# The second block's experts in a fixed order on TensorE, four at a time, with one sum for four experts

## The chip, the cores and the metric

The kernel runs on one core of one Trainium2 chip. A core has TensorE (matrix multiplication, PE in the profile; PEld is its weight load), VectorE (DVE), ScalarE (ACT), GpSimd (POOL), and SyncE (SP), which here starts the transfers from the chip's memory. The metric is the device time of one execution in microseconds (us); less is better.

## The reference

Two transformer-like blocks are run one after the other on 256 tokens of width 1024. The change lies in the last stage of the second block, its mixture of experts: each token chooses 2 of 32 experts, and each expert is a gated two-layer network with three float32 weight matrices (`w1`, `w3`: 1024 x 512; `w2`: 512 x 1024).

```python
def expert_block(args):
    xb, e = args
    hid = jax.nn.silu(xb @ w1[e]) * (xb @ w3[e])
    return hid @ w2[e]
...
out = jax.ops.segment_sum(ys * row_gate[:, None], row_tok, num_segments=T)
```

The result is scaled by a gate vector (`g2`), added to the token stream `h`, and a last root-mean-square norm gives the output.

## The kernel before

The token stream `x` lies in the on-chip memory as 8 tiles of 128 channels x 256 tokens. `experts2` goes over the 32 experts in pairs. All experts' weights are read, 6 MB for a pair, in tiles of 1 MB (128 x 2048 float32): four of `w1`, four of `w3`, four of `w2`. `S.load` takes them through a ring of buffers, one transfer on SP's queue for each, in the order of the program; a tile's transfer can start when the matmuls of the tile that held its buffer are done. The ring has 19 buffers in this stage: 4 of the whole program, 7 of the second block, and 8 that `block2` adds at its end with `S.extra_ring(8, S.ring_n)`.

For every four experts ("a group" below):

- `oh` (VectorE) holds one-hot columns that say which token stands in which of an expert's 64 places. `S.gather_parts` multiplies the token rows (kept as a sum of two parts, `u2h` and `u2l`) with `oh`: 32 matmuls `gx`, evacuated from the accumulators (PSUM) by ScalarE and VectorE into `xg`.

For every pair in the group:

- `G` and `U` (64 places x 512 for each of the two experts) take 16 matmuls each. The two experts use the two halves of the array's columns, so their matmuls are 128x64; in the trace each of them has two records.
- `hs` = silu(G) * U (ScalarE, then VectorE); four transposes to `hT` on TensorE, evacuated by VectorE.
- `sg`: the pair's columns of `oh` transposed (evacuated to `sel`), and the gates for its places (`gs`).
- `Yp`: the second layer in two halves `n` of 512 channels, with 8 matmuls (16 records) each; each half is evacuated to a high part `ysh` (ScalarE) and the rest `ysl` (VectorE), both times the gate.
- `add`: for each of the 8 channel tiles, two matmuls `cmb` bring the experts' rows back to their tokens, and VectorE adds the product to `x`.

The accumulators have 8 banks: two for `G`/`U`, two for `Yp`, two (`pt`) for `gx`, `sg` and `hT`, and two (`px`) for `cmb`. No order is written by hand: the framework's scheduler orders each engine's instructions when the program is built, and it may put a pair's `cmb` and the next group's `gx` among the matmuls of `Yp` and of the next pair's `G`. A matmul of 128x128 (`gx`, `cmb`, `sg`, `hT`) uses all columns of the array, one of 128x64 half of them.

In the last pair the squares of the finished tiles of `x` are summed at once (`sums.step`), and `last_norm` writes the output.

Of the kernel before, what the change touches and what calls it, by code (L numbers as in the profile page):

```python
# [173 lines left out]
class K:  # L174
# [123 lines left out]
    def across(self, out, r):  # L298

        for t in range(2):  # L300
            self.nc.tensor.matmul(out[:, 128 * t:128 * t + 128], bc(r[:, t:t + 1], [128, 128]), self.c("ident"), start=True, stop=True)
        return out[:, 0:256]
# [55 lines left out]
                self.split(hi[:, t, a], lo[:, t, a], o, nc.gpsimd)  # L358
        return hi, lo

    def gather_parts(self, pt, xt, oh, n, xg, A, B):

        nc = self.nc
        c = 512 // n
        for k in range(8):
            if k % c == 0:
                p = pt.tile([128, 512], F32, name="gx", tag="tp")
            q = p[:, n * (k % c):n * (k % c) + n]
            for i in range(4):
                nc.tensor.matmul(q, xt[i % 2][:, i // 2, 128 * k:128 * k + 128], oh[:, i // 2], start=(i == 0), stop=(i == 3))  # L370
# [77 lines left out]
def bc(ap, shape):  # L448
    return ap.to_broadcast(shape)
# [912 lines left out]
def block2(S, x):  # L1362

    nc, tc, I = S.nc, S.tc, S.I
    st = ExitStack()
    ring = S.extra_ring(1)
    h1 = S.pool("p2s", st=st, side="right")
# [19 lines left out]
    A = sb.tile([128, 8], F32, name="fgA")  # L1387
# [281 lines left out]
    for i in range(4):  # L1669
# [3 lines left out]
        for fb in range(2):  # L1673
# [43 lines left out]
def experts2(S, x, ring, out):  # L1717

    nc, tc, I = S.nc, S.tc, S.I
    st = ExitStack()  # L1720
    sb = S.pool("m2", st=st, side="right")
    C, V = S.c, S.v
    ident = C("ident")
    M = S.modT2
    CAP = S.cap
    B2 = M[:, 24:32, 0]

    def mm(o, l, r, a=True, b=True):
# [16 lines left out]
    r, ge = S.route  # L1745
# [61 lines left out]
    for e0 in range(0, 32, 2):  # L1807
        if e0 % 4 == 0:

            oh = lb.tile([128, 2, 4, 64], F32R, name="oh", bufs=1)  # L1810
            for t in range(2):
                nc.vector.tensor_tensor(oh[:, t], bc(pos[:, t, e0:e0 + 4, None], [128, 4, 64]), bc(C("iota")[:, None, 0:64], [128, 4, 64]), op=ALU.is_equal)
                if CAP < 64:
                    nc.vector.memset(oh[:, t, :, CAP:].bitcast(F32), 0.0)
            xg = lb.tile([128, 8, 256], F32, name="xg", bufs=1)
            S.gather_parts(pt, ut, oh.rearrange("p t e s -> p t (e s)"), 256, xg, S.A22, B2)
        if e0 == 0:

            nc.vector.tensor_scalar(og, pos, float(CAP), None, op0=ALU.is_gt)
            ov = lb.tile([128, 1], F32, name="ov")  # L1820
            nc.vector.tensor_reduce(ov, og, axis=AX.XY, op=ALU.add)
            nc.vector.tensor_tensor(og, og, gate, op=ALU.mult)
            p = pt.tile([128, 512], F32, name="ov", tag="tp")
            mm(p[:, 0:1], C("ones"), ov)
            nc.vector.tensor_copy(ovi, p[:, 0:1])
        c0 = e0 % 4
        G = pg.tile([128, 512], F32, name="G", tag="G")
        U = pg.tile([128, 512], F32, name="U", tag="G")
        for wn, p in (("w1", G), ("w3", U)):
            for k in range(0, 8, 2):  # L1830
                wt = S.load(I[wn][2 * e0 + k // 2], wn)
                for kk in range(2):
                    for e in range(2):
                        lo = 1024 * kk + 512 * e
                        mm(p[64 * e:64 * e + 64, :], xg[:, k + kk, 64 * (c0 + e):64 * (c0 + e) + 64], wt[:, lo:lo + 512], k + kk == 0, k + kk == 7)

        p = pt.tile([128, 512], F32, name="sg", tag="tp")
        ohp = [oh[:, t, c0:c0 + 2].rearrange("p e s -> p (e s)").bitcast(F32) for t in range(2)]
        for t in range(2):
            nc.tensor.transpose(p[:, 128 * t:128 * t + 128], ohp[t], ident)  # L1840
        for t in range(2):
            mm(p[:, 256:258], ohp[t], gate[:, t, e0:e0 + 2], t == 0, t == 1)
        sel = lb.tile([128, 256], F32R, name="sel", tag="h1", bufs=3)
        nc.scalar.copy(sel, p[:, 0:256])
        gs = lb.tile([128, 1], F32, name="gs", bufs=2)
        for e in range(2):
            nc.vector.tensor_copy(gs[64 * e:64 * e + 64, :], p[64 * e:64 * e + 64, 256 + e:257 + e])
        hs = lb.tile([128, 512], F32, name="hs", tag="h2", bufs=6)
        nc.scalar.activation(hs, G, AF.Silu)
        nc.vector.tensor_tensor(hs, hs, U, op=ALU.mult)  # L1850
        tp = pt.tile([128, 512], F32, name="hT", tag="tp")
        for b in range(4):
            nc.tensor.transpose(tp[:, 128 * b:128 * b + 128], hs[:, 128 * b:128 * b + 128], ident)
        hT = lb.tile([128, 4, 128], F32, name="hT", tag="h2", bufs=6)
        S.evac(hT.rearrange("p b i -> p (b i)"), tp, "v")

        def evac(n):

            hi, lo = (lb.tile([128, 512], F32R, name="ys" + a, tag="h2", bufs=6) for a in "hl")
            nc.scalar.mul(hi, Y[:, n, :], gs)  # L1860
            nc.vector.scalar_tensor_tensor(lo, Y[:, n, :], gs, hi.bitcast(F32), op0=ALU.mult, op1=ALU.subtract)
            return hi, lo

        def add(k, ys):

            pc = px.tile([128, 256], F32, name="cmb")
            b = 128 * (k % 4)
            for i, a in enumerate(ys):
                mm(pc, a[:, b:b + 128], sel, i == 0, i == 1)
            nc.vector.scalar_tensor_tensor(x[:, k, :], pc, M[:, 40 + k, 0:1], x[:, k, :], op0=ALU.mult, op1=ALU.add)  # L1870

        Y = py.tile([128, 2, 512], F32, name="Yp")
        last = e0 == 30
        if last:
            S.sqrt_ahead(hs[:, 0:1])
            sums = Sums(S, x, [pg.tile([128, 512], F32, name="tq", tag="G") for _ in range(2)], S.ones8(), lambda: lb.tile([128, 256], F32, name="tsq", tag="h1", bufs=3))
        for n in range(2):
            for q in range(0, 4, 2):
                wt = S.load(I["w2"][2 * e0 + 2 * n + q // 2], "w2")
                for b in range(2):  # L1880
                    for e in range(2):
                        lo = 1024 * b + 512 * e
                        mm(Y[64 * e:64 * e + 64, n, :], hT[:, q + b, 64 * e:64 * e + 64], wt[:, lo:lo + 512], q + b == 0, q + b == 3)
            ys = evac(n)
            if last and n:
                for k in range(4):
                    sums.step(k)
            for b in range(4):
                add(4 * n + b, ys)
                if last and 4 * n + b > 5:  # L1890
                    sums.step(4 * n + b - 2)
# [92 lines left out]
```

## Time and profile before

| | |
|---|---|
| time, median of 3 runs | 2150.25 us (2148.17 to 2151.69) |
| the profiled execution | 2152.28 us |
| its span, first to last instruction | 2150.1 us |
| TensorE busy, share of the span | 82% |
| VectorE, ScalarE, GpSimd busy | 33%, 21%, 10% |
| moved by transfers | 723.76 MB, mean 337 GB/s |

The profile is of one execution, whose time stands 2 us above both its own span and the median. A busy share is a mean over stages with different limits: the first block's experts (about 580 to 1250 us) and the stage of the change (about 1620 to 2140 us) are read apart below. A matmul's duration in the trace overlaps its neighbours', so what matmuls cost is read from the distance of their starts.

### The profile page before, as it was taken

To read this page: it belongs to the slowest core of one execution; us is meant where nothing else is said; L and a number is where in the kernel's file an instruction comes from. 1 tells how busy PE (TensorE), PEld (TensorE's weight loads), DVE (VectorE), ACT (ScalarE), POOL (GpSimd) and SP (SyncE) were. 2 spreads that over 40 slices of the span, in tenths; PEclk is the share of its full clock that TensorE was granted. 3 is DMA by queue.
4 is the path that set the end of the run, shared out by engine and by line. 5 is a ranking of instruction groups with operands and counts; after the bars stand their busy time and mean duration, and the time that the engine had idled before them with its cause. 6 is when DMAs were issued, how large, how long until landed. Compare 5 with 4: busy or idle time off the path is not lost.

```text
span 2150.1 us, 26014 instructions
## 1 busy us (share of the span) xinstructions
PE 1766.6 (82%) x10570; PEld 852.3 (40%) x10570; DVE 710.8 (33%) x1417; ACT 442.8 (21%) x791; POOL 216.2 (10%) x277
## 2 busy tenths in 40 slices
PE   6969998877666677677666678999998999999997
PEld 1647557411211112111211116899993433333333
DVE  4797673310001101111100115996552222222222
ACT  3623234200000001000100004676441111110111
POOL 2325422000000000000000002332020000000000
PEclk8989999786877777777887778999998999999998
DMA  7356559799999999999999996345587999999980
GB/s 307 129 196 255 195 205 407 312 424 424 424 424 425 425 424 425 425 424 424 424 425 424 423 422 243 125 158 229 182 308 290 417 410 386 398 392 384 398 331 21
DMA packets 120844, 723.76 MB, mean 337 GB/s; under 512 B 11456, under 2 KB 13248, under 8 KB 50448
## 3 DMA queue, kind: packets, MB, share of 16 engines
q1 hardware_dynamic: 119600, 717.97, 82.4%
q0 software_dynamic: 1120, 4.08, 0.5%
q8 instruction: 85, 1.39, 0.2%
q14 instruction: 39, 0.32, 0.0%
HBM read 720.96 MB, written 1.05 MB: 336 GB/s over the span
## 4 chain that ended last, share of the span: by engine, by line
PE 41%; DMA 41%; DVE 8%; issue 5%; ACT 3%; POOL 1%; SPq 0%; DVEq 0%; ACTq 0%; POOLq 0%
DMA w_up<-in_w_up_dram 14%; DMA w_gate<-in_w_gate_dram 13%; DMA w_down<-in_w_down_dram 12%; PE pj L253 7%; PE G L1729 6%; PE Yp L1729 6%; PE pw L253 2%; PE cmb L1729 2%; PE gx L370 2%; PE U L1729 2%; PE U L1179 2%; DVE tmp L781 1%; PE mp L514 1%; PE ya L253 1%; DMA w<-in_w_dram 1%
## 5 line engine op out<-in xcount | busy, mean ns | idle before, releaser
L1179 PE MATMUL U<-w_up,xg 128*32 128x512 f32 x1024 | 201.3, 875 | 99.5 <-DMA w_up<-in_w_up_dram 99.5
L1179 PE MATMUL Yp<-w_down,hT 128*32 128x512 f32 x1024 | 173.7, 786 | 84.6 <-DMA w_down<-in_w_down_dram 74.3
L1179 PE MATMUL G<-w_gate,xg 128*32 128x512 f32 x1024 | 162.8, 668 | 53.9 <-DMA w_gate<-in_w_gate_dram 53.6
L1285 DVE TENSOR_TENSOR hs<-hs,U 128x512 f32<-128x512 f32 x16 | 11.0, 688 | 469.6 <-PE U L1179 469.6
L1729 PE MATMUL Yp<-w,hT 128*64 128x512 f32 x512 | 136.3, 602 | 4.1 <-DVE hT L228 4.1
L1729 PE MATMUL G<-w,xg 128*64 128x512 f32 x512 | 138.5, 602 | 0.0
L1179 PEld LDWEIGHTS U<-w_up,xg 128*32 128x32 f32 x1024 | 25.0, 127 | 272.5 <-DMA w_up<-in_w_up_dram 240.3
L1729 PE MATMUL U<-w,xg 128*64 128x512 f32 x512 | 122.1, 592 | 0.0
L253 PE MATMUL pj<-uh,whi 128*128 128x256 f32 x408 | 118.2, 291 | 3.2 <-ACT uh L1409 3.2
L253 PE MATMUL pj<-uh,wlo 128*128 128x256 f32 x408 | 116.8, 286 | 1.1 <-DVE wlo L235 1.1
L253 PE MATMUL pj<-ul,whi 128*128 128x256 f32 x408 | 115.8, 284 | 0.0
L1179 PEld LDWEIGHTS Yp<-w_down,hT 128*32 128x32 f32 x1024 | 26.5, 124 | 207.1 <-DMA w_down<-in_w_down_dram 174.1
L1299 ACT COPY ys<-Yp 128x256 f32<-128x256 f32 x17 | 6.3, 372 | 480.6 <-DVE ys L1298 480.6
L234 ACT CAST whi<-win 128x1024 fp32r<-128x1024 f32 x72 | 75.0, 1046 | 97.8 <-PE pj L253 63.8
L1179 PE MATMUL cmb<-seln,ys 128*128 128x256 f32 x256 | 85.0, 467 | 11.7 <-DVE ys L1298 9.5
L1422 POOL DMA_DIRECT2D dist<-in_dist_dram x1 | 0.6, 606 | 910.7 <-PE tq L436 910.7
L1179 PEld LDWEIGHTS G<-w_gate,xg 128*32 128x32 f32 x1024 | 27.8, 114 | 150.6 <-DMA w_gate<-in_w_gate_dram 108.0
L1298 DVE COPY ys<-Yp 128x256 f32<-128x256 f32 x17 | 7.2, 425 | 242.2 <-PE Yp L1179 242.2
L1295 DVE SCALAR_TENSOR_TENSOR x<-cmb,modT,x 128x256 f32<-128x256 f32 x128 | 59.4, 483 | 68.0 <-PE cmb L1179 68.0
L253 PEld LDWEIGHTS pj<-uh,whi 128*128 128x128 f32 x408 | 77.6, 191 | 5.2 <-ACT uh L1409 3.5
L1179 PEld LDWEIGHTS cmb<-seln,ys 128*128 128x128 f32 x256 | 49.6, 218 | 75.6 <-DVE ys L1298 29.2
L253 PEld LDWEIGHTS pj<-uh,wlo 128*128 128x128 f32 x408 | 77.6, 190 | 2.5 <-DVE wlo L235 1.5
(565 smaller groups left out, 2986.2 us busy)
## 6 DMA issues: line engine op xcount, KB each, us to landing
w<-in_w_dram SPq DMA_DIRECT2D x192, 1024.0 KB, 8.4
w_gate<-in_w_gate_dram SPq DMA_DIRECT2D x128, 1024.0 KB, 19.6
w_up<-in_w_up_dram SPq DMA_DIRECT2D x128, 1024.0 KB, 19.6
w_down<-in_w_down_dram SPq DMA_DIRECT2D x128, 1024.0 KB, 19.6
wmod<-in_w_mod_dram SPq DMA_DIRECT2D x48, 1024.0 KB, 6.1
win<-in_w_in_dram SPq DMA_DIRECT2D x36, 1024.0 KB, 4.9
wout<-in_w_out_dram SPq DMA_DIRECT2D x8, 1024.0 KB, 5.8
wrnn<-in_w_rnn_out_dram SPq DMA_DIRECT2D x8, 640.0 KB, 7.3
```

What stands on the lines that cost most here:

```text
L234: self.nc.scalar.copy(hi, x)
L253: self.nc.tensor.matmul(out, a(k), b(k), start=(n == 0), stop=(n == 3 * K - 1))
L370: nc.tensor.matmul(q, xt[i % 2][:, i // 2, 128 * k:128 * k + 128], oh[:, i // 2], start=(i == 0), stop=(i == 3))
L514: nc.tensor.matmul(out, l, r, start=a, stop=b)
L781: nc.vector.tensor_tensor(tv, X[:, 0:i, 0:i], bc(Lt[:, None, 0:i, i], [128, i, i]), op=ALU.mult)
L1179: nc.tensor.matmul(out, l, r, start=a, stop=b)
L1285: nc.vector.tensor_tensor(hs, hs, U, op=ALU.mult)
L1295: nc.vector.scalar_tensor_tensor(x1[:, k, :], pc, S.modT[:, 40 + k, 0:1], x1[:, k, :], op0=ALU.mult, op1=ALU.add)
L1298: nc.vector.tensor_copy(ys[:, 0:256], Y[:, 0:256])
L1299: nc.scalar.copy(ys[:, 256:512], Y[:, 256:512])
L1422: nc.gpsimd.dma_start(dist, I["dist"])
L1729: nc.tensor.matmul(o, l, r, start=a, stop=b)
```

## The change

The scheduler no longer orders this stage on TensorE: every matmul and transpose goes through `keep_in_program_order`, so TensorE runs them as they are written. The loop goes over groups of four experts. The combination of a group's eight channel tiles is put off until the next group's first pair has its `G` and `U`, and runs in one go: four matmuls `cmb` for a channel tile (two pairs, two parts each) and one addition to `x` for four experts. The next group's gather runs in one go between the second pair's `U` and its `Yp`, around the transposes `hT`. `sg` is done once for the four experts. `hT` is evacuated by ScalarE. The ring loses one buffer (18 in this stage), whose room goes to more buffers for `ysh` and `ysl`. In the last group the first pair's sum is added in parts.

```diff
-    def gather_parts(self, pt, xt, oh, n, xg, A, B):
+    def gather_parts(self, pt, xt, oh, n, xg, A, B, ks=range(8), mm=None):
...
-    more = S.extra_ring(8, S.ring_n)
+    more = S.extra_ring(7, S.ring_n)
...
+    def pe(o, l, r, a=True, b=True):
+
+        tc.keep_in_program_order(nc.tensor.matmul(o, l, r, start=a, stop=b))
...
+    def tokens_of(oh, e0):
...
+        for c in range(2):
+            for t in range(2):
+                turned(p[:, 256 * c + 128 * t:256 * c + 128 * t + 128], ohp[c][t])
+        for c in range(2):
+            for t in range(2):
+                pe(pq[:, 2 * c:2 * c + 2], ohp[c][t], gate[:, t, e0 + 2 * c:e0 + 2 * c + 2], t == 0, t == 1)
...
-        S.evac(hT.rearrange("p b i -> p (b i)"), tp, "v")
+        S.evac(hT.rearrange("p b i -> p (b i)"), tp, "s")
...
-        def add(k, ys):
+    def add(k, pairs):
+
+        pc = px.tile([128, 256], F32, name="cmb")
+        b = 128 * (k % 4)
+        L = [(a, sel) for ys, sel in pairs for a in ys[k // 4]]
+        for i, (a, sel) in enumerate(L):
+            pe(pc, a[:, b:b + 128], sel, i == 0, i == len(L) - 1)
+        nc.vector.scalar_tensor_tensor(x[:, k, :], pc, M[:, 40 + k, 0:1], x[:, k, :], op0=ALU.mult, op1=ALU.add)
...
+    for e0 in range(0, 32, 4):
+        last = e0 == 28
+        hs = gate_up(xg, e0, 0)
+        sel, gs = tokens_of(oh, e0)
...
+        hT = across(hs)
+        if before:
+            for k in range(8):
+                add(k, before)
         Y = py.tile([128, 2, 512], F32, name="Yp")
...
+        for n in range(2):
+            down(Y, hT, e0, n)
+        ya = [evac(Y, n, gs[:, 0:1]) for n in range(2)]
+        hs = gate_up(xg, e0, 1)
         if not last:
+            oh = one_hot(e0 + 4)
+            xg = lb.tile([128, 8, 256], F32, name="xg", bufs=1)
+            rows(oh, xg, (0, 1))
+            hT = across(hs)
+            rows(oh, xg, range(2, 8))
+            Y = py.tile([128, 2, 512], F32, name="Yp")
+            for n in range(2):
+                down(Y, hT, e0 + 2, n)
+            before = [(ya, sel[:, 0]), ([evac(Y, n, gs[:, 1:2]) for n in range(2)], sel[:, 1])]
             continue
```

`gate_up` (G, U, `hs`), `across` (`hT`), `down` (`Yp`) and `evac` hold the code of before. In the listings of the order below a line number is that of the kernel listed, `w_` and a number is one weight tile, and "x4" counts instructions in a row.

TensorE in the kernel before, late in the stage, from the first pair's transposes on:

```order
L1853 MATMUL hT<-cst,hs 128x128 x4
L1840 MATMUL sg<-cst,oh 128x128 x2
L1729 MATMUL sg<-gate,oh 128x2 x2
L1729 MATMUL Yp<-w_12082,hT 64x512 x4
L1729 MATMUL Yp<-w_12088,hT 64x512 x4
L1729 MATMUL cmb<-sel,ysh 128x256 x2
L1729 MATMUL cmb<-sel,ysl 128x256 x2
L1729 MATMUL Yp<-w_12114,hT 64x512
L1729 MATMUL cmb<-sel,ysh 128x256
L1729 MATMUL cmb<-sel,ysl 128x256
```

TensorE in the changed kernel, at the first pair of a group:

```order
L1809 MATMUL U<-w_10711,xg 64x512 x4
L1812 MATMUL sg<-cst,oh 128x128 x4
L1809 MATMUL cmb<-gate,oh 128x2 x4
L1812 MATMUL hT<-cst,hs 128x128 x4
L1809 MATMUL cmb<-sel,ysh 128x256
L1809 MATMUL cmb<-sel,ysl 128x256
```

Behind it 30 more `cmb` of the same two kinds follow, and then all 16 `Yp`; `cmb` no longer stands between the halves of `Yp`, and a weight tile's four matmuls are no longer parted.

VectorE in the kernel before, one pair late in the stage (`x_105` is `x`):

```order
L1861 SCALAR_TENSOR_TENSOR ysl<-Yp,gs,ysh 128x512
L1870 SCALAR_TENSOR_TENSOR x_105<-cmb,modT_76,x_105 128x256 x4
L1861 SCALAR_TENSOR_TENSOR ysl<-Yp,gs,ysh 128x512
L1870 SCALAR_TENSOR_TENSOR x_105<-cmb,modT_76,x_105 128x256 x4
L1850 TENSOR_TENSOR hs<-hs,U 128x512
L228 COPY hT<-hT 128x512
```

VectorE in the changed kernel, one whole group:

```order
L1858 TENSOR_TENSOR hs<-hs,U 128x512
L1842 COPY gs<-cmb 64x2 x2
L1818 TENSOR_TENSOR oh<-pos,cst 128x256 x2
L1892 SCALAR_TENSOR_TENSOR x_105<-cmb,modT_76,x_105 128x256 x8
L1882 SCALAR_TENSOR_TENSOR ysl<-Yp,gs,ysh 128x512 x2
L1858 TENSOR_TENSOR hs<-hs,U 128x512
L372 TENSOR_SCALAR xg<-gx,A_9894,modT_76 128x256 x4
L1882 SCALAR_TENSOR_TENSOR ysl<-Yp,gs,ysh 128x512 x2
```

The eight additions stand behind the making of the next group's `oh`, which has moved ahead of them, and there are 8 for a group in place of 16.

## Rows read from the trace of the kernel before

**Rows 1.** Windows (us): length, five engines' busy time, TensorE clock, DMA share, GB/s.

```profile
580.00:1230.00 650.00, 451.25 (x2400) 103.86 (x2392) 64.02 (x129) 33.16 (x78) 0.00 (x0) 0.78 1.02 424
...
1640.00:1700.00 60.00, 59.07 (x272) 23.88 (x270) 15.95 (x34) 6.95 (x12) 0.00 (x0) 1.00 1.00 407
...
1640.00:2090.00 450.00, 426.80 (x1958) 173.25 (x1956) 114.12 (x244) 48.35 (x86) 0.00 (x0) 1.00 0.97 395
```

**Rows 2.** SP's own waits, 1640 to 2090 us: total us, times, longest us.

```profile
SPq L216 <- PE Yp L1729: 168.8, 51, 6.7
```

**Rows 3.** All engines' waits, same stretch: TensorE's only wait for a weight tile.

```profile
PE cmb L1729 <- DMA w<-in_w_dram: 2.3, 3, 0.8
```

**Rows 4.** Chain that ended last: the evacuation of second pairs' `hT`, six groups apart.

```profile
1733.09 0.70 DVE hT L228
...
2119.22 0.70 DVE hT L228
```

**Rows 5.** Timeline of TensorE in one group: start, busy us, instruction, count, wait.

```profile
1862.37 1.94 PE L1729 MATMUL Yp<-w,hT 128*64 128x512 f32 x8 [0.30 <-DVE hT L228]
1864.24 0.39 PE L370 MATMUL gx<-oh,u2h 128*128 128x256 f32 x1
1864.46 0.28 PE L370 MATMUL gx<-oh,u2l 128*128 128x256 f32 x1
1864.58 0.28 PE L370 MATMUL gx<-oh,u2h 128*128 128x256 f32 x1
...
1865.02 1.94 PE L1729 MATMUL Yp<-w,hT 128*64 128x512 f32 x8
...
1894.65 0.66 PE L1853 MATMUL hT<-cst,hs 128*128 128x128 f32 x4 [0.85 <-DVE hs L1850]
...
1900.54 0.50 PE L1729 MATMUL cmb<-sel,ysh 128*128 128x256 f32 x2 [0.79 <-ACT ysh L1860]
1901.32 0.50 PE L1729 MATMUL cmb<-sel,ysl 128*128 128x256 f32 x2 [0.28 <-DVE ysl L1861]
1901.75 1.07 PE L1729 MATMUL Yp<-w,hT 128*64 128x512 f32 x2
1902.76 0.39 PE L1729 MATMUL cmb<-sel,ysh 128*128 128x256 f32 x1
...
1907.85 0.50 PE L1729 MATMUL cmb<-sel,ysh 128*128 128x256 f32 x2 [0.78 <-ACT ysh L1860]
...
1909.72 1.08 PE L1729 MATMUL G<-w,xg 128*64 128x512 f32 x4
1910.73 0.39 PE L1729 MATMUL cmb<-sel,ysh 128*128 128x256 f32 x1
```

**Rows 6.** Timeline: an addition to `x`, and a `cmb` that waits for one.

```profile
1901.75 0.88 DVE L1870 SCALAR_TENSOR_TENSOR x<-cmb,modT,x 128x256 f32<-128x256 f32 x2 [0.48 <-PE cmb L1729]
...
2134.07 0.88 DVE L1870 SCALAR_TENSOR_TENSOR x<-cmb,modT,x 128x256 f32<-128x256 f32 x2 [0.48 <-PE cmb L1729]
2134.61 0.38 PE L1729 MATMUL cmb<-sel,ysh 128*128 128x256 f32 x1 [0.46 <-DVE x L1870]
```

**Rows 7.** Timeline at the stage's start: first gather, and SP's first refill of the ring.

```profile
1619.78 0.55 PE L370 MATMUL gx<-oh,u2h 128*128 128x256 f32 x1 [0.98 <-DVE oh L1812]
1628.63 0.33 SPq L216 DMA_DIRECT2D w<-in_w_dram  x1
```

**Rows 8.** Timeline at the end: the last pair's `U`, and the output's scaling.

```profile
2110.24 7.45 PE L1729 MATMUL U<-w,xg 128*64 128x512 f32 x31
2140.63 3.22 DVE L1738 SCALAR_TENSOR_TENSOR o<-x,vec,rrow 128x256 f32<-128x256 f32 x8 [1.32 <-PE rrow L301]
```

**Rows 9.** First block's experts, where TensorE waits for weights: two tiles, and a window.

```profile
1226.68 1.06 PE L1179 MATMUL Yp<-w_down,hT 128*32 128x512 f32 x8 [0.66 <-DMA w_down<-in_w_down_dram]
1235.47 1.93 PE L1179 MATMUL Yp<-w_down,hT 128*32 128x512 f32 x8 [0.50 <-DMA w_down<-in_w_down_dram]
1235.00:1240.00 5.00, 3.87 (x16) 0.40 (x16) 0.00 (x0) 0.00 (x0) 0.00 (x0) 0.50 1.03 428
```

More of the change, by code (lines that the diff above doesn't have):

```diff
@@ L359, in token_parts @@
         return hi, lo
-    def gather_parts(self, pt, xt, oh, n, xg, A, B):
+    def gather_parts(self, pt, xt, oh, n, xg, A, B, ks=range(8), mm=None):
         nc = self.nc
         c = 512 // n
-        for k in range(8):
+        for k in ks:
             if k % c == 0:
@@ L369, in gather_parts @@
             for i in range(4):
-                nc.tensor.matmul(q, xt[i % 2][:, i // 2, 128 * k:128 * k + 128], oh[:, i // 2], start=(i == 0), stop=(i == 3))
+                mm(q, xt[i % 2][:, i // 2, 128 * k:128 * k + 128], oh[:, i // 2], i == 0, i == 3)
             if k % 2:
@@ L1735, in last_norm @@
         for k in range(0, 8, 2):
-            o = so.tile([128, 2, 256], F32, name="o", tag="h2", bufs=6)
+            o = so.tile([128, 2, 256], F32, name="o", tag="h2", bufs=8)
             for c in range(2):
@@ L1806, in experts2 @@
     px = S.pool("m2c", 2, True, pst)
-    for e0 in range(0, 32, 2):
-        if e0 % 4 == 0:
-            oh = lb.tile([128, 2, 4, 64], F32R, name="oh", bufs=1)
-            for t in range(2):
[L1812 to L1826, printed above, removed]
+    def pe(o, l, r, a=True, b=True):
+        tc.keep_in_program_order(nc.tensor.matmul(o, l, r, start=a, stop=b))
@@ new lines, in turned, with one_hot, rows @@
+    def turned(o, i):
+        tc.keep_in_program_order(nc.tensor.transpose(o, i, ident))
+    def one_hot(e0):
+        oh = lb.tile([128, 2, 4, 64], F32R, name="oh", bufs=1)
+        for t in range(2):
+            nc.vector.tensor_tensor(oh[:, t], bc(pos[:, t, e0:e0 + 4, None], [128, 4, 64]), bc(C("iota")[:, None, 0:64], [128, 4, 64]), op=ALU.is_equal)
+            if CAP < 64:
+                nc.vector.memset(oh[:, t, :, CAP:].bitcast(F32), 0.0)
+        return oh
+    def rows(oh, xg, ks):
+        S.gather_parts(pt, ut, oh.rearrange("p t e s -> p t (e s)"), 256, xg, S.A22, B2, ks, pe)
@@ new lines, in tokens_of @@
+    def tokens_of(oh, e0):
+        p = pt.tile([128, 512], F32, name="sg", tag="tp")
+        pq = px.tile([128, 256], F32, name="cmb")
+        ohp = [[oh[:, t, 2 * c:2 * c + 2].rearrange("p e s -> p (e s)").bitcast(F32) for t in range(2)] for c in range(2)]
+        for c in range(2):
+            for t in range(2):
+                turned(p[:, 256 * c + 128 * t:256 * c + 128 * t + 128], ohp[c][t])
+        for c in range(2):
+            for t in range(2):
+                pe(pq[:, 2 * c:2 * c + 2], ohp[c][t], gate[:, t, e0 + 2 * c:e0 + 2 * c + 2], t == 0, t == 1)
+        sel = lb.tile([128, 2, 256], F32R, name="sel", bufs=2)
+        nc.scalar.copy(sel.rearrange("p c t -> p (c t)"), p)
+        gs = lb.tile([128, 2], F32, name="gs", bufs=2)
+        for e in range(2):
+            nc.vector.tensor_copy(gs[64 * e:64 * e + 64, :], pq[64 * e:64 * e + 64, 0:4].rearrange("p (c e) -> p c e", e=2)[:, :, e])
+        return sel, gs
@@ L1834, in experts2 @@
                         lo = 1024 * kk + 512 * e
[L1835 to L1848, printed above, removed]
+                        pe(p[64 * e:64 * e + 64, :], xg[:, k + kk, 128 * c + 64 * e:128 * c + 64 * e + 64], wt[:, lo:lo + 512], k + kk == 0, k + kk == 7)
@@ L1849, in experts2, with across @@
+        hs = lb.tile([128, 512], F32, name="hs", bufs=1)
         nc.scalar.activation(hs, G, AF.Silu)
         nc.vector.tensor_tensor(hs, hs, U, op=ALU.mult)
+        return hs
+    def across(hs):
         tp = pt.tile([128, 512], F32, name="hT", tag="tp")
         for b in range(4):
-            nc.tensor.transpose(tp[:, 128 * b:128 * b + 128], hs[:, 128 * b:128 * b + 128], ident)
-        hT = lb.tile([128, 4, 128], F32, name="hT", tag="h2", bufs=6)
-        S.evac(hT.rearrange("p b i -> p (b i)"), tp, "v")
@@ L1857, in evac @@
[L1857 to L1862, printed above, removed]
-        def add(k, ys):
[L1866 to L1870, printed above, removed]
+            turned(tp[:, 128 * b:128 * b + 128], hs[:, 128 * b:128 * b + 128])
@@ new lines, in across, with down @@
+        hT = lb.tile([128, 4, 128], F32, name="hT", bufs=1)
+        S.evac(hT.rearrange("p b i -> p (b i)"), tp, "s")
+        return hT
+    def down(Y, hT, e, n, qs=(0, 2)):
+        for q in qs:
+            wt = S.load(I["w2"][2 * e + 2 * n + q // 2], "w2")
+            for b in range(2):
+                for i in range(2):
+                    lo = 1024 * b + 512 * i
+                    pe(Y[64 * i:64 * i + 64, n, :], hT[:, q + b, 64 * i:64 * i + 64], wt[:, lo:lo + 512], q + b == 0, q + b == 3)
@@ new lines, in evac @@
+    def evac(Y, n, g):
+        hi, lo = (lb.tile([128, 512], F32R, name="ys" + a, tag="h2", bufs=8) for a in "hl")
+        nc.scalar.mul(hi, Y[:, n, :], g)
+        nc.vector.scalar_tensor_tensor(lo, Y[:, n, :], g, hi.bitcast(F32), op0=ALU.mult, op1=ALU.subtract)
+        return hi, lo
+    def add(k, pairs):
[5 more added lines that the diff above has]
+        nc.vector.scalar_tensor_tensor(x[:, k, :], pc, M[:, 40 + k, 0:1], x[:, k, :], op0=ALU.mult, op1=ALU.add)
@@ new lines, in experts2 @@
+    oh = one_hot(0)
+    xg = lb.tile([128, 8, 256], F32, name="xg", bufs=1)
+    rows(oh, xg, range(8))
+    nc.vector.tensor_scalar(og, pos, float(CAP), None, op0=ALU.is_gt)
+    ov = lb.tile([128, 1], F32, name="ov")
+    nc.vector.tensor_reduce(ov, og, axis=AX.XY, op=ALU.add)
+    nc.vector.tensor_tensor(og, og, gate, op=ALU.mult)
+    before = None
+    for e0 in range(0, 32, 4):
+        last = e0 == 28
+        hs = gate_up(xg, e0, 0)
+        sel, gs = tokens_of(oh, e0)
+        if e0 == 0:
+            p = pt.tile([128, 512], F32, name="ov", tag="tp")
+            pe(p[:, 0:1], C("ones"), ov)
+            nc.vector.tensor_copy(ovi, p[:, 0:1])
+        hT = across(hs)
+        if before:
+            for k in range(8):
+                add(k, before)
@@ L1872, in experts2 @@
         Y = py.tile([128, 2, 512], F32, name="Yp")
[L1873 to L1876, printed above, removed]
         for n in range(2):
[L1878 to L1891, printed above, removed]
@@ new lines, in experts2 @@
+        S.sqrt_ahead(hs[:, 0:1])
+        sums = Sums(S, x, [pg.tile([128, 512], F32, name="tq", tag="G") for _ in range(2)], S.ones8(), lambda: lb.tile([128, 256], F32, name="tsq", tag="h2", bufs=8))
+        add(4, [(ya, sel[:, 0])])
+        hT = across(hs)
+        for k in range(5, 8):
+            add(k, [(ya, sel[:, 0])])
+        Y = py.tile([128, 2, 512], F32, name="Yp")
+        down(Y, hT, 30, 0)
+        yb = [evac(Y, 0, gs[:, 1:2])]
+        down(Y, hT, 30, 1, (0,))
+        for k in range(4):
+            add(k, [(ya, sel[:, 0]), (yb, sel[:, 1])])
@@ L1894, in experts2 @@
+        down(Y, hT, 30, 1, (2,))
+        yb.append(evac(Y, 1, gs[:, 1:2]))
+        for k in range(4):
+            sums.step(k)
+        for k in range(4, 8):
+            add(k, [(yb, sel[:, 1])])
+            if k > 5:
+                sums.step(k - 2)
         for k in (6, 7):
```

4 lines of the change are left out of this document (3 added, 1 removed).

## The prediction

> **What bounds the kernel now.** I read the windows first. The reader is to compare two stages. In the first block's experts the transfers move 424 GB/s for 650 us, at a DMA share of 1.02, with TensorE busy for 451 of 650 us: that stage hangs on the transfers. In the stage of the change they move 395 GB/s, with TensorE busy for 427 of 450 us at the full granted clock [rows 1]. The waits say who holds whom: SP stands for 168.8 us behind the matmuls of `Yp` alone, as a transfer needs a buffer that TensorE still reads, while TensorE's only listed wait for a weight tile is 2.3 us in 450 [rows 2, 3]. So here TensorE sets the pace, and the transfers stand 7% under what they do elsewhere.
>
> The chain gives the pace: from one second pair's `hT` to that of six groups later it is 386.1 us, 64.4 us a group [rows 4]. A group needs 24 tiles of 1.0486 MB, 25.17 MB; at 424 GB/s that is 59.4 us, or 2.47 us a tile. So however fast TensorE gets, at most 5.0 us of 64.4 can be had while the transfers are the other limit.
>
> **What the change takes from TensorE, per group.** The matmuls are the same in number. What goes is time between them, read in the timeline of one group [rows 5].
>
> Torn tiles. Two records of `Yp` alone occupy 1.01 us (1901.75 to 1902.76), and four records of `G` also 1.01 (1909.72 to 1910.73), where eight take 1.87 (1862.37 to 1864.24): four more cost 0.86. A matmul without its neighbour in the other half of the columns costs as much as the two together. The old order puts `cmb` or `gx` inside four tiles of a group, and each makes one such step more: 4 x 0.86 = 3.4 us gone.
>
> Excursions, that is leaving 128x64 matmuls for 128x128 ones and coming back. Eight records are 1.72 and take 1.87, so 0.15 on the way out; five `gx` take 0.78 where their spacing of 0.12 makes 0.60, so 0.18 on the way back: 0.33. I count 14 excursions in an old group and 4 in a new one: 10 x 0.33 = 3.3 us.
>
> Waits. `hT` waits 0.85 for `hs` in each pair; the new order puts `sg` there in the first pair and eight `gx` (about 1 us) in the second. `Yp` waits 0.30 for `hT`; now `cmb` or 24 `gx` (2.9 us) cover it. `cmb` waits 0.79 and 0.28 for `ysh` and `ysl`, and again 0.78; they are now a pair of experts older. I take two, one and all of these: 1.7 + 0.3 + 1.85 = 3.9 us.
>
> Added: eight additions stand in a row. A `cmb` of a channel tile is four matmuls, 0.48; its addition starts about 0.43 after the start of the last matmul before it (1901.32 to 1901.75), takes 0.44, and the next use of that bank can start 0.1 later [rows 5, 6]. One bank's round is 0.36 + 0.43 + 0.44 + 0.10 = 1.33, and there are two banks, so 0.67 for a channel tile instead of 0.48: 8 x 0.19 = 1.5 us lost. The old trace has no such row of eight; the bounds are 0 (matmuls alone) and 8 x 0.85 = 6.8 (banks that don't alternate). I take 1.5, as the tail's `cmb` did restart with its own bank's addition, 0.10 behind it, while the other ran [rows 6]. `oh` now stands ahead of the additions on VectorE (0.8 us), but `sg`, `gs` and `hT` on TensorE cover it; without that cover it would cost 0.8. ScalarE's evacuation of `hT` lies beside `cmb` or `gx`. Half of the additions go (8 x 0.44 a group), from an engine that nobody waits for longer than shown: nothing.
>
> Sum: 64.4 - 3.4 - 3.3 - 3.9 + 1.5 = 55.3 us a group. **That is below the 59.4 of the transfers, so the transfers become the limit.**
>
> **The new end, by the transfers.** From 1640 to 2090 us they moved 395 x 450 = 177.8 MB [rows 1]. The missing buffer means one tile fewer by 1640. Against that, SP's first refill, at 1628.63, waited for the first `G` tile, whose matmuls stood among the `gx`; with all 32 `gx` first, from 1619.78 on, I put their end at 1625.3 (an estimate: half of them twice 0.12 us apart, since the first ones of rows 7 are longer than those of rows 5, half 0.12 apart) and that tile's, eight records, at 1627.2: 1.4 us sooner [rows 5, 7], worth 0.6 MB. So 178.3 MB remain, and at 424 GB/s the last tile lands at 1640 + 420.5 = 2060.5, where before the transfers ran until almost 2090. Why 424: nothing but free buffers differs between the stages in what is asked of them, and a full queue is what the first one has. Bounds: 424, and the 407 that this stage showed at a share of 1.00 [rows 1], by which it would be 2078.1.
>
> The page "DMA: Bandwidth & Descriptors" of the Trainium skill, section Specifications, gives about 358 GB/s as a core's share of the memory. By it these bytes would take 498 us and the change could bring nothing; the rows stand above it in both stages, so the measurement decides and it gets no chance.
>
> TensorE must now be followed to the same end. Gather until 1625.3; `G` and `U` of the first pair are 64 records, 13.8 us at 0.215; then about 4 us (an estimate from the waits above) for `sg`, `hT` and its evacuation, which no `cmb` covers in the first group; `Yp` 6.9; the second pair's `G` and `U` 13.8: done at about 1664. Seven groups of 55.3 make 2051. The last `U` tile is four tiles before the last one: it lands at 2060.5 - 9.9 = 2050.6, and its records take 1.7 us: 2052.3. Both meet there; the later one counts.
>
> From the last record of `U` (2110.24 + 7.45 - 0.59 = 2117.1) to the span's end it was 33.0 us, the output's scaling within it [rows 8]. The new tail has the same sums and norm; the waits for `ysh` and `ysl` after the first half are covered by half of the second, a torn tile goes, and `hT` waits as before: I take 1 us less, 32.0. Span: 2052.3 + 32.0 = 2084.3, 65.8 less than 2150.1. The profiled execution took 2152.28, so 2086.5; the median of the runs stands 2.0 below it: **2084.5, say 2085 us**, 3.0% less.
>
> **Rivals.**
> *TensorE stays the bound* (0.2). If a group costs more than 55.5, each microsecond more costs seven. At the upper bound of the additions (6.8 for 1.5) it is 60.6: `U` ends at 1664 + 7 x 60.6 = 2088, and the time is 2120; half way, at 58, it is 2102. For it: a fixed order can't step around a late tile, and one wait that I missed repeats in every group. Against: each wait in rows 5 has its cover named above.
> *The transfers stay below 424* (0.15). At 407 the end is 17.6 later: 2102. For it: the share was already 0.97 to 1.00 here. Against: 424 held for 650 us.
> *The change doesn't do what it says* (0.03): the 395 GB/s is all that these reads give, and TensorE now waits for tiles instead: 2148 to 2153. Against it stand SP's waits [rows 2].
> *Slower* (0.04), by the clock. Once TensorE has used up its lead it waits at each tile, as it does in the first block's experts. There the granted clock is 0.78 on the mean, in places 0.50 (1.2 of 2.4 GHz), and eight records then take 1.93 us instead of 1.06 [rows 1, 9]. At 0.78 over all eight groups a group is 55.3 / 0.78 = 70.9, and the time 2150 + 8 x 6.5 = 2202. It decides at a mean of 55.3 / 64.4 = 0.86. Against it: of 192 tiles 22 would have landed by 1640 and 32 by 1664, where TensorE has used 20; this lead of 12 shrinks by 24 - 55.3 / 2.47 = 1.6 tiles a group, so waits come only near the end; and at half clock a tile takes longer than its transfer, which ends the waiting.
> The Trainium skill warns of this in "TensorE: Matmul & The Clock Gate", section HAM oscillation: matmul bursts shorter than the wait for the next transfer keep the clock at half rate. By that rule alone the slower time above would come; the trace agrees for the first block's experts.
>
> **How the numbers follow.** My forecast, the transfers as the limit at 424, has 0.58 (own range 2077 to 2094). The low end is 2077: my estimates of the start (1.4) and of the tail (1) can each be some 4 us too small. The high end of the range is 2106, which takes in both middle rivals at their likely price and leaves out TensorE's upper bound, no gain and the clock. Faster by over 0.2% (about 4 us, what this measurement can tell): 0.58 + 0.2 + 0.15 = 0.93; within it 0.03; slower 0.04.
>
> **What would show it.** Right: between 1640 us and the last transfer the windows show 420 GB/s or more; the last weight tile lands at about 2061 instead of 2088; groups take 55 us early on and 59 later; TensorE's waits name the weight tiles in the last two groups. The torn tiles and the waits of `cmb` for `ysh` are gone from its timeline, and eight `cmb` groups take 5.4 us. Wrong: groups over 57 us with SP still behind TensorE (additions or `gx` cost more than I say); windows at 400 GB/s with SP never waiting (transfers); or a granted clock below 0.9 in the stage.

## The result and the profile after

The changed kernel takes **2104.28 us** (median of 4 runs, 2101.58 to 2105.51) against 2149.21 for the kernel before in the same session: a ratio of 0.9781, 95% interval 0.9769 to 0.9794, or 2.2% less. The forecast was 2085 us, in a range of 2077 to 2106. The direction and the place of the gain were right; of the 65 us forecast, 45 came. The profiled execution took 2101.58 us, with a span of 2099.5. One of four executions of e6_torn (below) took 4661 us, far from the other three, and is left out of its time.

The windows of the changed kernel, in the columns of [rows 1]:

```profile
1640.00:2050.00 410.00, 385.41 (x1986) 171.43 (x1984) 80.59 (x158) 57.06 (x93) 0.00 (x0) 1.00 1.01 426
...
2060.00:2070.00 10.00, 9.22 (x48) 3.84 (x46) 2.44 (x5) 1.67 (x3) 0.00 (x0) 1.00 0.15 64
```

The transfers do what was forecast: 426 GB/s where they did 395. The 64 GB/s of the last row are 0.64 MB, 1.5 us at full rate, which makes 2061.5 (forecast, by the same full rate: 2060.5); in fact the rate falls at the end, and the last bytes come between 2062 and 2063 (131 GB/s there, none after). SP still stands behind TensorE, for half the time of [rows 2] (410 us here, 450 there). Its longest wait is now for the transfers themselves, in a row that the kernel before does not have:

```profile
SPq L216 <- DMA w<-in_w_dram: 196.1, 105, 2.8
SPq L216 <- PE Yp L1809: 87.8, 38, 10.2
```

TensorE's own timeline gives its pace. The first `sg` stands at the same place of each group (here of the second and of the eighth):

```profile
1695.50 0.66 PE L1812 MATMUL sg<-cst,oh 128*128 128x128 f32 x4
...
2038.11 0.66 PE L1812 MATMUL sg<-cst,oh 128*128 128x128 f32 x4
```

Six groups in 342.6 us are **57.1 us a group**, where 64.4 stood before [rows 4] and 55.3 was forecast. By the prediction's own sign ("groups over 57 us with SP still behind TensorE") its first rival came true: TensorE stays the bound. The transfers run at their full rate all the same: at 426 GB/s they need 59 us for a group's tiles, and TensorE, at 57.1, lives from the tiles that it has in the ring. Which of the two sets the end can't be read from the pace alone; e4_ring5 below tests it. What TensorE waits for between 1640 and 2050 us is new:

```profile
PE gx L1809 <- ACT xg L374: 18.5, 28, 0.7
PE gx L1809 <- DVE xg L372: 1.9, 7, 0.3
PE cmb L1809 <- DVE x L1892: 1.8, 6, 0.3
```

The waits for `hs`, `ysh` and `ysl` are gone, as forecast. In their place the gather waits 28 times, four times in each of seven groups. The timeline of all engines at the start of one gather:

```profile
1894.96 0.28 PE L1809 MATMUL gx<-oh,u2l 128*128 128x256 f32 x1
1895.28 0.57 ACT L374 ACTIVATE xg<-gx,modT,A 128x256 f32<-128x256 f32 x1 [6.93 <-PE gx L1809]
1895.90 0.39 PE L1809 MATMUL gx<-oh,u2h 128*128 128x256 f32 x1 [0.66 <-ACT xg L374]
...
1896.75 0.54 DVE L372 TENSOR_SCALAR xg<-gx,A,modT 128x256 f32<-128x256 f32 x1 [1.38 <-PE gx L1809]
```

A bank holds two channel tiles of the gather. The fourth matmul of the first starts at 1894.96. The fifth writes the other half of the same bank; it starts at 1895.90, as soon as ScalarE has read the first half, and not 0.12 later. So each bank loses 0.82 us on TensorE. VectorE's evacuation of the second half holds TensorE only once a group, for 0.27 us (the second of the three waits above), where `hT` has taken the other bank. In the old order these matmuls stood between those of `Yp` [rows 5], which filled the time.

### The profile page after: what moved, and what is told of

It reads as the page before. It is cut to its first block, busy times and chain, and to the rows that moved or that the text cites. A ratio compares the mean times of both kernels' runs of the same rounds, so it can differ in the third digit from the quotient of the medians.

```text
span 2099.5 us, 25845 instructions
## 1 busy us (share of the span) xinstructions
PE 1716.2 (82%) x10570; PEld 849.8 (40%) x10570; DVE 675.1 (32%) x1325; ACT 452.3 (22%) x799; POOL 215.7 (10%) x277
## 3 DMA queue, kind: packets, MB, share of 16 engines
HBM read 720.96 MB, written 1.05 MB: 344 GB/s over the span
## 4 chain that ended last, share of the span: by engine, by line
PE 43%; DMA 41%; DVE 9%; ACT 3%; issue 2%; POOL 1%; SPq 0%; DVEq 0%; ACTq 0%; POOLq 0%
DMA w_up<-in_w_up_dram 14%; DMA w_gate<-in_w_gate_dram 13%; DMA w_down<-in_w_down_dram 13%; PE pj L253 7%; PE Yp L1809 5%; PE G L1809 5%; PE U L1809 5%; PE pw L253 2%; PE gx L1809 2%; DVE tmp L781 1%; PE cmb L1809 1%; PE ya L253 1%; PE mp L514 1%; PE U L1179 1%; PE yb L253 1%
## 5 line engine op out<-in xcount | busy, mean ns | idle before, releaser
L1179 PE MATMUL G<-w_gate,xg 128*32 128x512 f32 x1024 | 164.5, 677 | 55.3 <-DMA w_gate<-in_w_gate_dram 55.1
L1809 PE MATMUL Yp<-w,hT 128*64 128x512 f32 x512 | 113.8, 596 | 2.2 <-DVE ysl L1882 1.6
L1809 PE MATMUL G<-w,xg 128*64 128x512 f32 x512 | 114.0, 598 | 0.0
L1809 PE MATMUL U<-w,xg 128*64 128x512 f32 x512 | 112.6, 592 | 0.0
```

What stands on the lines that cost most here:

```text
L1179: nc.tensor.matmul(out, l, r, start=a, stop=b)
L1809: tc.keep_in_program_order(nc.tensor.matmul(o, l, r, start=a, stop=b))
```

## Experiments

The theory: this wait keeps TensorE at 57.1 us a group; without it the transfers, which need 59 for 24 tiles, set the end. Rivals: the transfers or the ring set it already (A); the row of additions holds the group (B). Groups are read as above, between the first `sg` of neighbouring groups. The runs come from four sessions, in which the kernel before took 2149 to 2153 us, so runs of different sessions are compared by their ratio.

| run | a group, us | time, us | ratio to before (95%) |
|---|---|---|---|
| changed kernel | 57.10 | 2104.3 | 0.9781 (0.9769 to 0.9794) |
| e1_gather | 54.42, last 59.22 | 2088.2 | 0.9698 (0.9680 to 0.9716) |
| e3_gx4 | 52.93, last 60.11 | 2086.9 | 0.9692 (0.9675 to 0.9710) |
| e2_cmb4 | 55.86 | 2092.5 | 0.9719 (0.9702 to 0.9736) |
| e4_ring5 | 57.10 | 2104.7 | 0.9771 (0.9751 to 0.9791) |
| e5_spread | 56.78 | 2100.0 | 0.9768 (0.9752 to 0.9785) |
| e6_torn | 58.80 | 2112.9 | 0.9826 (0.9807 to 0.9846) |
| e13_even | 58.53 | 2111.5 | 0.9821 (0.9806 to 0.9837) |
| e14_odd | 61.98 | 2138.7 | 0.9941 (0.9926 to 0.9956) |
| e7_free | 61.49 | 2126.7 | 0.9893 (0.9877 to 0.9910) |
| e11_pairwise | 59.77 | 2127.3 | 0.9902 (0.9879 to 0.9925) |
| e10_all4 | 51.6, last 59.17 | 2083.2 | 0.9683 (0.9669 to 0.9696) |
| e15_all_ring5 | 51.6, last 59.57 | 2088.2 | 0.9706 (0.9693 to 0.9720) |

**The gather's wait, taken away in two ways.** e1_gather moves the evacuations behind both halves:

```diff
             if k % 2:
-                nc.vector.tensor_scalar(xg[:, k, :], q, ...)
-            else:
-                nc.scalar.activation(xg[:, k, :], q, ...)
+                nc.scalar.activation(xg[:, k - 1, :], p[:, 0:256], ...)
+                nc.vector.tensor_scalar(xg[:, k, :], q, ...)
```

> The eight matmuls of a gather bank stand in a row and both evacuations come after them; nothing else changes. Theory (TensorE is held at 57.1 us a group by its wait, in every bank of the gather, for ScalarE to empty the bank's first half): the four waits of about 0.8 us go, the gather block falls from 8.7 to about 5.6 us and the group to about 54.0, which is below the transfers' 59. TensorE then waits for tiles near the end, and the time is about 2091 us (2087 to 2095): the last U tile, which lands about 2052, followed by the same tail. Rival A (the transfers, or the ring of buffers, set the end already): 2104, within 2 us. Rival B (the additions hold the group): the waits in the gather only move on to another place, group over 56.5 and time over 2100.

e3_gx4 leaves the order and gives each channel tile a bank:

```diff
-            q = p[:, n * (k % c):n * (k % c) + n]
+            q = px.tile([128, 256], F32, name="gx", tag="cmb") if k % 2 else pt.tile([128, 512], F32, name="gx", tag="tp")[:, 0:256]
```

> Each channel tile of the gather in a bank of its own, four banks in turn (two of them those of the combine, which is idle then); order of matmuls and evacuations as in the changed kernel. Theory (the wait comes from writing the second half of a bank whose first half is still read): no wait left, gather block about 5.2 us, time as with the evacuations behind both halves, about 2091 us. Rival C (the engines that empty the banks are too slow for a gather in a row, whichever banks are used): the waits come back as waits for banks, block over 7.5 us, time over 2099. Rival A: 2104.

Both came out as the theory has it, a little below 2091: the group falls by 2.7 and by 4.2 us. e1_gather keeps a rest, two waits a group of the gather's banks for `hT` and `xg`; in e3_gx4 the gather waits for nothing, and rival C falls with it. Its two halves are two tiles in two banks, so it doesn't show which of the two, the tile or the bank, makes the wait. In the last groups (two in e3_gx4, one in e1_gather) the pace is the transfers' 59 to 60, and TensorE waits for tiles. The timeline of TensorE in e3_gx4, three tiles of `U`:

```profile
1896.47 1.94 PE L1807 MATMUL U<-w,xg 128*64 128x512 f32 x8 [0.55 <-DMA w<-in_w_dram]
1898.96 1.94 PE L1807 MATMUL U<-w,xg 128*64 128x512 f32 x8 [0.56 <-DMA w<-in_w_dram]
1901.39 1.94 PE L1807 MATMUL U<-w,xg 128*64 128x512 f32 x8 [0.49 <-DMA w<-in_w_dram]
```

The starts are 2.4 to 2.5 us apart, one transfer's time.

**The additions.** e2_cmb4 takes `pc` from `px` and `pt` in turn:

```diff
-        pc = px.tile([128, 256], F32, name="cmb")
+        pc = px.tile([128, 256], F32, name="cmb") if k % 2 else pt.tile([128, 512], F32, name="cmb", tag="tp")[:, 0:256]
```

> The combine's sums of the channel tiles alternate over four banks in place of two; the gather is left as in the changed kernel. Theory: the three gaps of about 0.4 us in each row of eight go, a group falls from 57.1 to about 55.8 us and the time to about 2095 (2092 to 2098). Rival B (the additions are what holds the group): the row falls by 2 us or more and the time below 2091. Rival A (transfers): 2104.

The group loses 1.24 us, the gaps alone; the gather's waits stay. Rival B falls. Seven such steps and a tail of 32.7 in place of 33.9 make 10 us of trace; the ratios differ by 0.62%, 13 us, and their intervals leave room for that.

**Who sets the end.** Two buffers fewer, once in the changed kernel and once in the one with the waits removed:

```diff
-    more = S.extra_ring(7, S.ring_n)
+    more = S.extra_ring(5, S.ring_n)
```

> Two weight buffers fewer (the last extra ring of 5 in place of 7). Theory (TensorE holds the stage up to the end; it has a lead of about 12 us over the last U tile): the transfers end some 5 us later and the time stays at 2104, within 2 us. Rival A (the transfers set the end): two tiles of 2.46 us later, about 2109.

> The kernel with all three edits, with two weight buffers fewer. Theory (the transfers are its limit): two tiles of 2.46 us that can't be fetched ahead come at the end: 4.9 us more, about 2089.5. Rival (TensorE is still the bound): no change, as in the changed kernel with two buffers fewer.

In the changed kernel the groups and the time stay, though the transfers end later: between 2072 and 2073 us, 10 us later, of which some 4 are a later start of the stage. In the other the time rises by 5.0 us (2083.2 to 2088.2), two tiles, and the groups at the transfers' pace begin one group sooner. The two answers show the change of limit: TensorE in the changed kernel, the transfers once the waits are out. Rival A falls.

**Torn tiles.** e5_spread puts two `add` ahead of each of the first pair's four down tiles; e6_torn puts them after the tile's first matmul.

```diff
-        if before:
-            for k in range(8):
-                add(k, before)
...
+                    if inside and not b and not i:
+                        inside()
```

> The eight additions of a group, two at a time, stand ahead of the four down tiles of the first pair in place of all ahead of the first; every tile is left whole. Theory: three more excursions of 0.33 us each (+1.0), and the gaps of the additions' banks (1.3 in a row of eight) are covered by the tiles between: 57.1 becomes about 56.8 us a group, the time about 2102 (2097 to 2107). Rival D (an excursion costs much more than 0.33): each microsecond a group gives seven, 2110 or more.

> As the kernel with the additions spread two at a time, but each two stand after the first matmul of their down tile and not ahead of it, so that four tiles of a group are torn. Theory (a matmul without its neighbour in the other half of the columns costs as much as the two): 4 x 0.86 = 3.4 us a group more than with whole tiles, seven groups 24 us: about 2126 (2120 to 2132). Rival E (the tear costs nothing, what the prediction put down to it is the excursion): the same as with whole tiles, about 2102.

e5_spread's group is the 56.8 expected, and rival D falls. e6_torn's is 2.0 longer, not 3.4. Its timeline shows 2, 8, 8, 8 and 6 records between the additions: a tile's last three matmuls pair up with the first of the next tile, so that only one pair is lost in all (0.86), and the first `Yp` now waits 0.73 for `hT` with no addition to cover it; one stretch more makes up the rest. The cut had been counted by tiles, where it has to be counted by stretches. So the cost was measured again with eight stretches of even length, ahead of every second matmul (`range(0, 16, 2)`), and of 1 and 3 matmuls in turn (`(0, 1, 4, 5, 8, 9, 12, 13)`):

> The eight additions stand one at a time ahead of every second matmul of the first pair's down tiles, so that these come in eight stretches of two matmuls (the two halves of the columns). Theory: four excursions more than with the additions two at a time ahead of whole tiles (56.78 us a group there), 4 x 0.33 = 1.3: 58.1 us a group, about 2109 us (2106 to 2112).

> The same eight additions and eight stretches, but of one and three matmuls in turn, so that in each tile two matmuls stand without their neighbour. Theory now (a stretch with an odd number of half matmuls takes as long as with one more, 0.43 a record pair, and cuts that leave even stretches cost only the excursion): four pairs of odd stretches, 4 x 0.86 = 3.4 us a group more than with stretches of two, 61.5 us, about 2133 us. Rival E (the halves' pairing costs nothing): as with stretches of two, 2109.

TensorE's timeline, without the additions between them, first of e13_even, then of e14_odd:

```profile
1932.85 1.08 PE L1809 MATMUL Yp<-w,hT 128*64 128x512 f32 x4
```

```profile
1951.22 1.07 PE L1809 MATMUL Yp<-w,hT 128*64 128x512 f32 x2 [0.26 <-ACT hT L230]
...
1952.90 1.93 PE L1809 MATMUL Yp<-w,hT 128*64 128x512 f32 x6
```

One matmul (x2) takes what two take (x4), and three (x6) what four take (x8, [rows 5]). The groups differ by 3.45 us, 0.86 for each of four odd pairs: the first price of the prediction. Rival E falls. Four excursions more, e13_even against e5_spread, cost 1.75, of which 0.26 is the wait for `hT`: 0.37 each, for 0.33 in the prediction. Both times are some microseconds over those expected, e14_odd's by 5.7; its groups explain 3.4 of that.

**The two halves of the change.** e7_free leaves the order to the scheduler (`pe` and `turned` without `keep_in_program_order`); e11_pairwise keeps it and adds each pair by itself:

```diff
             hT = across(hs)
+            for k in range(8):
+                add(k, [(ya, sel[:, 0])])
             rows(oh, xg, range(2, 8))
...
-            before = [(ya, sel[:, 0]), ([evac(Y, n, gs[:, 1:2]) for n in range(2)], sel[:, 1])]
+            before = [([evac(Y, n, gs[:, 1:2]) for n in range(2)], sel[:, 1])]
```

> The changed kernel's groups of four and sums of four, without the fixed order on TensorE: the order is again chosen by the program that schedules. Theory (the fixed order's gain is the torn tiles and excursions, 6.7 us a group, and its price the waits of the gather in a row, about 3.6): about 3.1 us a group slower, 22 us in all: 2126 (2110 to 2140). Rival F (the regrouping brought the gain, the order nothing): 2104, within 4. Rival G (the free order covers the gather's waits and tears little): below 2100.

> The fixed order with one sum for each pair of experts again: eight sums of two matmuls for the second pair in their place of the changed kernel, and eight for the first pair in the gather, behind hT. Theory (a row of additions is set by its two banks, not by its matmuls: 0.24 + 0.43 + 0.44 + 0.10 = 1.2 us a bank's round, 0.6 a channel tile): each row costs some 4.9 us where the row of four matmuls costs 5.2, so a group grows by about 4.6 us and the time to about 2136 (2125 to 2142). Rival H (the matmuls alone set it): 2 x 8 x 0.24 = 3.8 us in place of 5.2, the time falls to about 2096.

The free order takes 2126.7, the 2126 of the theory, and rivals F and G fall: the gain divides evenly, 1.1% (some 23 us) by all but the order (the regrouping, with `hT` on ScalarE and one buffer fewer, which no run parts), 1.1% more by the fixed order. That the time came out to the microsecond is partly luck. The group, read in the last four, is 4.4 us longer and not 3.1, while the early groups and the tail are shorter than put; and its timeline has twelve stretches of 128x64 matmuls in a group but tears only one pair (2 and 14 records), not four. Its waits on TensorE, 1640 to 2050 us, are the old ones, and the gather's are mostly filled:

```profile
PE cmb L1809 <- ACT ysh L1881: 7.9, 10, 0.8
PE hT L1812 <- DVE hs L1858: 4.3, 5, 0.9
PE gx L1809 <- ACT xg L374: 3.3, 5, 0.7
```

Pairwise sums cost 2.67 us a group more: less than the 4.6 expected, well away from rival H. (The time, 23 us longer, has 4 more than seven groups explain; its four executions spread from 2121 to 2133.) The banks' round is shorter than put, and the added row covers a wait of 0.27 in the gather behind `hT`. TensorE's timeline of e11_pairwise, one bank's turn to the other's:

```profile
1942.10 0.38 PE L1809 MATMUL cmb<-sel,ysh 128*128 128x256 f32 x1 [0.75 <-DVE x L1892]
...
1943.27 0.36 PE L1809 MATMUL cmb<-sel,ysh 128*128 128x256 f32 x1 [0.28 <-DVE x L1892]
...
1944.32 0.38 PE L1809 MATMUL cmb<-sel,ysh 128*128 128x256 f32 x1 [0.25 <-DVE x L1892]
```

Two channel tiles in 1.05 to 1.17 us, whose matmuls alone need 0.48: with two matmuls each, the row goes at the pace of its banks; with four it stands 1.24 us over its matmuls (e2_cmb4).

**All three edits.** e10_all4 has e3_gx4, e2_cmb4, and the two halves of a down result as two accumulators:

```diff
-        Y = py.tile([128, 2, 512], F32, name="Yp")
+        Y = [py.tile([128, 512], F32, name="Yp", tag=f"Y{n}") for n in range(2)]
```

> Gather with each channel tile in one of four banks, the combine's sums over four banks too, and the two halves of a down result as two accumulators, so that in the tail the second half doesn't wait for the first half's evacuation (1.6 us). Theory (with the gather's waits gone the transfers set the end, so the combine's banks bring nothing more in the groups): 1.6 us from the tail and up to 0.7 from its additions: 2084.5 us (2082 to 2086). Rival (TensorE is still the bound in most groups): 1.3 us a group more, below 2079.

2083.2 us, 1.0% below the changed kernel (the intervals 0.9669 to 0.9696 and 0.9769 to 0.9794 stand apart) and the fastest here. Against e3_gx4 the gain is within the intervals, as expected: groups of 51.6 us only bring TensorE to the transfers' pace sooner.

The third edit also shows what a wait goes by. ScalarE's evacuations of the two halves, in the changed kernel (where `Yp` runs from 1759.54 to 1766.63) and, below the dots, in e10_all4 (1740.92 to 1748.01):

```profile
1766.67 0.69 ACT L1881 ACTIVATE ysh<-Yp,gs 128x512 fp32r<-128x512 f32 x1 [11.45 <-PE Yp L1809]
1768.18 0.69 ACT L1881 ACTIVATE ysh<-Yp,gs 128x512 fp32r<-128x512 f32 x1 [0.82 <-DVE ysl L1882]
...
1744.62 0.69 ACT L1879 ACTIVATE ysh<-Yp,gs 128x512 fp32r<-128x512 f32 x1 [6.69 <-PE Yp L1807]
```

The halves lie in two banks in both. As one tile, the first half waits for the matmuls of both, and ScalarE's reading of the second for VectorE's reading of the first; as two tiles, the first half is read while the second is still being multiplied. So in this program the order is kept for the tile, and a bank of its own is not enough if the tile is shared.

## Why the prediction was right in direction and off in size

**What held.** TensorE was the bound (the 2.3 us of [rows 3] too stand at `cmb`, which reads no weight tile); the change gave the transfers 426 GB/s; by full rate the last tile came 1.0 us behind the forecast. That last is partly luck: SP's first refill came at 1630.52, not 1627.2, and 426 GB/s in place of 424 made up for 2 of these 3.3 us. The torn tiles' 3.4 us a group (3.45 measured), the 1.5 of the row of additions (1.24) were right, and the waits of `hT`, `Yp` and `cmb` that it named are gone from the groups.

**What did not.** The forecast, with the transfers as the limit, had a range of its own of 2077 to 2094, and 2104.28 lies outside it. It lies within the stated 2077 to 2106 because that range took in two rivals, of which the one on TensorE came true.

**The step that failed** is the sum of 55.3 us a group, and in it the sentence "each wait in rows 5 has its cover named above". That list held the waits of the old order only. Its covers were "24 `gx` (2.9 us)" at 0.12 us a matmul; but a gather in a row can't run at 0.12, because in `gather_parts` the evacuation of a bank's first half stands ahead of the matmuls of the second. In the old order other matmuls stood there, so no row showed it. Measured, it is 4.2 us a group (57.10 to 52.93 in e3_gx4: four times 0.82, and the rest around the wait for VectorE behind `hT`), which the sum lacked. The page "PSUM — Partial Sum Buffer" of the Trainium skill, section Terms, has two engines at the same bank and the same 32 partitions at once as an error; by it the wait can be covered or moved to another bank, and not just left out. The trace has the second half waiting each time in these seven groups, which fits; but as the waits also go by the tile (e10_all4), it doesn't show the bank to be their cause, and no run tried the matmuls without the wait.

The sum missed by 1.8 and not by 4.2, because the excursions were undercounted: an old group has 14 stretches of 128x64 matmuls, a new one two and not four, as `Yp`, `G` and `U` follow each other. Twelve excursions of 0.37 are 4.4 us for the 3.3 put down. With that, 64.4 - 3.4 - 4.4 - 3.9 + 1.2 + 4.2 is 58.1; that the group is 1.0 us shorter stays open. (One candidate: a wait costs more than its idle time, in the gather 0.82 for 0.66, and the sum took its six old waits at their idle time. At 0.16 each they would make 1.0; this is an estimate that no run tested.) In the price of the additions, 0.43 was read from the first of two matmuls, not from the last (1901.32 starts a row of two), which may be why the pairwise rows were shorter than put. "Half of the additions go: nothing" was wrong too for a fixed order, where the additions are on TensorE's path (2.67 us a group by e11_pairwise).

**From the group to the end.** The second `U` was to be done at 1664; it was at 1666.0, as the first gather took 11.2 us for 5.5, in a stage that began 3.9 sooner. Seven groups of 57.1 give 2065.7; the last `U` ends at 2065.6, 13.3 later than forecast, and about 12 later than its last tile allows (2061.5 less four tiles, plus 1.7). The tail was 33.9 for 32.0 (34.4 from the start of the last record, from where the prediction's 33.0 is taken): TensorE's timeline there shows a wait that was not foreseen, as the second half of `Yp` shares its tile with the first.

```profile
2068.47 3.65 PE L1809 MATMUL Yp<-w,hT 128*64 128x512 f32 x16
2073.70 1.94 PE L1809 MATMUL Yp<-w,hT 128*64 128x512 f32 x8 [1.57 <-DVE ysl L1882]
```

Together 15.2 us, the difference of the spans (2099.5 and 2084.3).

**The rivals.** That TensorE stays the bound, at 0.2, was the case, through a cause that it left unnamed ("one wait that I missed repeats in every group"). With a group of 57.1 in its own sum, the prediction would have had 2096; the start and the tail add 3.9, and the median stands 2.7 above the profiled execution where it was put 2.0 below. That a lower clock makes it slower did not come, not even where TensorE does catch up with the transfers (below).

## What to carry to other kernels

Before a row of matmuls is put in a fixed order, look at what its evacuations do to it: a wait that other work filled before has no row in the old trace, so read it off the program as well (which accumulator tile does the next matmul write, and who still reads it). Give matmuls of one half of the array's columns an even number in each stretch, and count stretches, not tiles. When one limit is 8% above the next, a gain pays only up to that next limit; two buffers fewer show in one run which of the two is in force.

## What the hardware showed that was not expected

Two half-column matmuls pair up across tiles: a stretch costs 0.86 us for each pair begun and 0.15 more in all (x2 and x4 1.01, x6 and x8 1.86), whichever weight tile they read.

The clock in the first gather depended on its waits. Windows of the changed kernel, then of e3_gx4:

```profile
1616.00:1622.00 6.00, 4.69 (x19) 4.10 (x20) 1.17 (x5) 1.13 (x2) 0.00 (x0) 0.50 0.01 3
1622.00:1624.00 2.00, 1.34 (x6) 1.05 (x6) 0.38 (x1) 0.57 (x1) 0.00 (x0) 0.50 0.00 0
1624.00:1627.00 3.00, 2.34 (x11) 1.95 (x9) 0.54 (x1) 1.63 (x2) 0.00 (x0) 0.50 0.00 0
```

```profile
1616.00:1622.00 6.00, 5.02 (x23) 4.92 (x24) 2.57 (x12) 1.13 (x2) 0.00 (x0) 0.50 0.01 3
1622.00:1624.00 2.00, 2.00 (x17) 1.90 (x16) 1.09 (x2) 0.90 (x2) 0.00 (x0) 0.96 0.00 0
```

With the waits the clock stayed at 0.50 (1.2 of 2.4 GHz) for the whole gather; without them it rose within it, and the gather took 5.7 us (1618.37 to 1624.03), not 11.2 (1615.92 to 1627.13). It was so in all kernels with the fixed order: in the eight with these waits the gather took 11.2 us each at 0.50, in the four without them 5.6 to 6.1, with the clock rising within it. So a wait of 0.66 us cost more than itself here.

Once at the transfers' pace, TensorE waits some 0.5 us at a tile of 1.94 in e10_all4, and its clock stayed at 1.00. The window of e10_all4:

```profile
1640.00:2040.00 400.00, 382.80 (x1994) 165.50 (x1990) 79.43 (x154) 58.29 (x95) 0.00 (x0) 1.00 1.01 426
```

In the first block's experts the clock stood at 0.50 with such waits [rows 9], but TensorE's timeline of the kernel before shows that they are what is left once it has fallen:

```profile
904.49 1.07 PE L1179 MATMUL G<-w_gate,xg 128*32 128x512 f32 x8 [1.46 <-DMA w_gate<-in_w_gate_dram]
906.91 1.94 PE L1179 MATMUL U<-w_up,xg 128*32 128x512 f32 x8 [1.36 <-DMA w_up<-in_w_up_dram]
909.25 1.94 PE L1179 MATMUL U<-w_up,xg 128*32 128x512 f32 x8 [0.40 <-DMA w_up<-in_w_up_dram]
...
914.12 1.06 PE L1179 MATMUL U<-w_up,xg 128*32 128x512 f32 x8 [0.50 <-DMA w_up<-in_w_up_dram]
```

At full clock (1.00 from 902 to 906 us) a tile there takes 1.07 and waits 1.4; then the clock falls (0.53 on the mean from 907 to 914), a tile of the same size takes 1.94 and waits 0.4 to 0.5, and the clock rises again (1.00 from 914 to 916.5). In the stage of the change a tile takes 1.94 at full clock. The rule in "TensorE: Matmul & The Clock Gate" of the Trainium skill, section HAM oscillation, is about bursts shorter than the wait; the trace agrees with it in both stages. So the prediction's "by that rule alone the slower time above would come" does not follow: here the burst is longer than the wait.
